# Order of the last products and place of the zero writes in a one-core transformer block

## The chip, the cores and the metric

The kernel runs on one core of one Trainium2 chip. Times are device microseconds of that core from start to end, over several runs; a profiled execution beside them leaves a trace of every instruction.

## The reference, cut to what matters

One layer on 1024 tokens of width 1024, in float32:

```
q, k, v, u = split(x @ w_in)
a = differential attention(q, k, v)      # 4 heads, softmax pairs, chunk-causal
s = S5 state-space mixer(u) with a gate  # 32 groups of 16 channels, 64 states each
h = layernorm(alpha * x + concat(a, s) @ w_out)
moe[t] = sum over the 2 experts chosen for t of  w * (silu(h @ w_gate) * (h @ w_up)) @ w_down
out = layernorm(alpha * h + moe)         # 32 experts, 4 groups, top 2 of one group
```

## The kernel before

Tokens lie in eight tiles of 128 rows (P = 128). Products are done in pairs of halves: a float32 operand is split into a high part (a cast on ACT) and a low part (a subtraction on DVE or POOL), and three products of the parts are added in PSUM.

The stages follow each other: projection of u and the constants of the state-space mixer (to some 75 us); the state-space units, with the projections of q, v and k filled in between them (`ssm_pair`, line 640); attention with the gate of the mixer and the loading of `w_out` filled in; output projection, first layernorm and routing (`route`); the 32 experts, one after the other; the last layernorm over the eight tiles.

Storage: 25 slots of 8 KB per partition are handed out by `Slots` (line 52), first released, first taken. A tile that takes a slot waits for the last reader of the slot's former tile.

Order: up to the first gather of expert rows, each engine's instructions are put in order by a planner, which simulates the program with costs of its own and issues on each engine what is ready, the earlier in the program first. From that gather on `keep_order` (line 1335) pins every engine to the order of the program. The queues of DMA issues on SP and POOL are ordered in the same way.

The zeros: the experts scatter their rows into `moe_dram`, two rows per token (2048 rows of 4 KB, 8 MB). Rows that no expert writes have to be zero. A memset on POOL (line 910) fills a tile of 128 by 1024, and four DMAs on SP's queue (line 912) write it to the 2048 rows, after attention unit 13 (`ZERO`).

The tail: experts 30 and 31 aren't scattered. Their rows are added to the sum by products with a choosing matrix. For each token tile i there are:

- `so_far` (line 1367): a load of the tile's rows of `moe_dram` by SP, then an accumulating load of its second rows by POOL, into `mos[i]`;
- `total(i)` (line 1440): the sum so far goes into PSUM by products with the identity (line 1449), then the products for expert 30 are added (line 1459);
- `add_late(i, 1)` (line 1452): the products for expert 31 (line 1455);
- `moments(i, step)` (line 1461): mean and variance. For a tile marked A in `NORM` ACT reads the sum out of PSUM (line 1472) and makes a square pass (line 1476); for a tile marked V DVE takes statistics from PSUM (line 1469). POOL makes the reciprocal root;
- `normed_rows(i, step)` (line 1481): two passes on DVE, then the tile's DMA to the output.

PSUM has eight banks: a tag `bank_pair` of two buffers of two banks each, a tag `bank0` with two buffers, and two single banks, `bank2` and `bank3`. An A tile takes a `bank_pair` buffer; a V tile takes two single banks: tile 0 both buffers of `bank0`, tile 7 `bank2` and `bank3`. Expert 31's y is in `bank0` too.

Of the kernel before, what the change touches and what calls it, by code (L numbers as in the profile page):

```python
# [11 lines left out]
F32 = mybir.dt.float32  # L12
# [7 lines left out]
P = 128  # L20
D = 1024
T = 1024
NT = T // P
# [9 lines left out]
NONE = 4096  # L33
ORDERED = (mybir.EngineType.PE, mybir.EngineType.Activation, mybir.EngineType.DVE, mybir.EngineType.Pool,
           mybir.EngineType.SP)
NORM = 'VAAAAAAV'
ZERO = 13
GB = 0
ASK, GLU, WO = (6, 12), (15, 16, 1, 20, 21, 1), (22, 24, 26, 30)
FILLS = [(ASK[0], ("ask", 2)), (ASK[1], ("ask", 3))]  # L40
for half in range(2):
    a, b, c = GLU[3 * half:3 * half + 3]
# [72 lines left out]
def tile_kernel(ctx: ExitStack, tc: tile.TileContext, I: dict, out: bass.AP, dbg=None):  # L115
    nc = tc.nc
    V, S, G, PE, SP = nc.vector, nc.scalar, nc.gpsimd, nc.tensor, nc.sync
# [7 lines left out]
    sl = Slots()  # L125
# [5 lines left out]
    def bank(name, which=0):  # L131

        if which == 1:
            turn[0] ^= 1
            which = 2 + turn[0]
        return psum.tile([P, 512], F32, tag=f"bank{which}", name=name, bufs=1 if which else 2)

    def bank2(name):
        return psum.tile([P, 1024], F32, tag="bank_pair", name=name, bufs=2)
# [6 lines left out]
    moe_dram = dram.tile([2 * T, D], F32, name="moe_dram")  # L146
# [13 lines left out]
    def add(out_, a, b, eng=V):  # L160
        return eng.tensor_tensor(out=out_, in0=a, in1=b, op=ALU.add)  # L161
# [110 lines left out]
    UTs, zT, qr, vv = {}, {}, {}, {}  # L272
# [265 lines left out]
    def wk(name, shape, bufs=1):  # L538
        return areas[where[name]].get(name, shape[1:], bufs=bufs, parts=shape[0])
# [59 lines left out]
    def ssm_unit(u, UT, z2, made):  # L599

        uo = 4 * (u % 2)
        Wm, Tm, M, C, Sn = made

        pz = bank(f"pz{u}", 1)
        for g in range(4):
            PE.matmul(pz[:, g * P:(g + 1) * P], Wm[:, g, :], UT[:, uo + g, :], start=True, stop=True)
        pz3 = pz.rearrange("p (g b) -> p g b", g=4)
        r1 = wk("r1", [P, 4, P])
        r2 = wk("r2", [P, 4, P])
        mul(r1, pz3, C)  # L610
        mul(r2[0:64], pz3[64:P], Sn[0:64])
        mul(r2[64:P], pz3[0:64], Sn[64:P])
        add(r1, r1, r2)
        Gs = wk("Gs", [P, 4, P])
        for g in range(4):
            V.tensor_tensor_scan(out=Gs[:, g, :], data0=r8[:, 4 * u + g:4 * u + g + 1].broadcast_to([P, P]),
                                 data1=r1[:, g, :], initial=0.0, op0=ALU.mult, op1=ALU.add)
        Gw = wk("r2", [P, 4, P])
        S.copy(Gw[0:64], Gs[64:P])
        S.copy(Gw[64:P], Gs[0:64])  # L620
        mul(Gs, Gs, C)
        mul(Gw, Gw, Sn)
        sub(H[:, :, 1:P], Gs[:, :, 0:P - 1], Gw[:, :, 0:P - 1])
        py = bank(f"py{u}")
        for g in range(4):
            o = py.rearrange("p (t g c) -> p t g c", g=4, c=16)[:, :, g, :]
            PE.matmul(o, UT[:, uo + g, :], Tm[:, :, g, :], start=True, stop=False)
            PE.matmul(o, H[:, g, :], M[:, g, :, :].rearrange("p t c -> p (t c)"), start=False, stop=True)

        y2 = wk("r1", [P, 512])  # L630
        k0 = math.sqrt(2.0 / math.pi)
        S.activation(y2, py, AF.Square, scale=math.sqrt(k0 * 0.044715))
        stt(y2, y2, k0, py, ALU.add, ALU.mult)
        S.activation(y2, y2, AF.Tanh)
        stt(z2[:, :, 16 * uo:16 * uo + 64], y2.rearrange("p (t n) -> p t n", t=8), 1.0,
            py.rearrange("p (t n) -> p t n", t=8), ALU.add, ALU.mult)
# [3 lines left out]
    def ssm_pair(c4, fill):  # L640
        z2 = wk("z2", [P, 8, P])
        if c4 % 2 == 0:
            zT[c4 // 2] = sl.get([P, 2, T], F32, f"zT{c4 // 2}")
        UT = UTs[c4 // 2][:, c4 % 2, :, :]
        for u in (2 * c4, 2 * c4 + 1):
            if u + 1 < NG // 4:
                made[u + 1] = ssm_prepare(u + 1)
            if u + 2 == NG // 4:
                spp.close()
                areas[0].close()  # L650
            ssm_unit(u, UT, z2, made.pop(u))
            if u + 2 == NG // 4:
                areas[1].close()
            fill(u)
        if c4 % 2 == 1:
            sl.put(UTs.pop(c4 // 2))
        for tq in range(2):
            pz = bank(f"zt{c4}{tq}", tq)
            for t_ in range(4):
                PE.transpose(pz[:, t_ * P:(t_ + 1) * P], z2[:, 4 * tq + t_, :], ident)  # L660
            S.mul(zT[c4 // 2][:, c4 % 2, :].rearrange("p (b t) -> p t b", t=8)[:, 4 * tq:4 * tq + 4, :],
                  pz.rearrange("p (t b) -> p t b", t=4), 0.5)
# [25 lines left out]
    def proj_k(h):  # L688
# [6 lines left out]
        sub(t_[64:P, 1, :], o[64:P, :], t_[0:64, 1, :].bitcast(F32))  # L695
        kk[h] = t_

    fills = [(proj_q, 0), (proj_q, 1), (proj_q, 2), (proj_q, 3), (proj_v, 0), (proj_v, 1), (proj_v, 2), (proj_v, 3)]
    made[0] = ssm_prepare(0)
    for c4 in range(4):  # L700
        ssm_pair(c4, lambda u: fills[u][0](fills[u][1]))
# [158 lines left out]
    def start(u):  # L860
        h, i = units[u]
        if i // 4 not in aoT:
            aoT[i // 4] = sl.get([P, NH, 512], F32, f"aoT{i // 4}")
        if (h, i // 4) not in grp:
            grp[h, i // 4] = (sm("L", 8, 4).rearrange("p (j c) -> p j c", c=2),
                              sm("RL", 8, 4).rearrange("p (j c) -> p j c", c=2), bank(f"po{h}_{i}", 1))
        live[u] = scores(h, i, qd[h], grp[h, i // 4][0], i % 4)
        starts[h] = starts.get(h, 0) + 1
        if starts[h] == NT:
            sl.put(*qd.pop(h), kk.pop(h))  # L870
# [23 lines left out]
    for u, (h, i) in enumerate(units):  # L894
        if u + LEAD < len(units):
            start(u + LEAD)
        L_, RL_, po_ = grp[h, i // 4]
        weigh(h, i, live.pop(u), L_, RL_, i % 4, po_)
        if u in late:
            late.pop(u)()  # L900
        ends[h, i // 4] = ends.get((h, i // 4), 0) + 1
        if ends[h, i // 4] == 4:
            late[u + LATE] = normalize(h, i // 4, po_, RL_)
        if u in fills:
            for f_, *a_ in fills[u]:
                {"ask": ask, "pre": glu_prepare, "glu": glu, "wo": wo_part}[f_](*a_)
        if u == ZERO:

            zero = sl.get([P, D], F32, "zero")
            G.memset(zero, 0.0)  # L910
            for j in range(4):
                SP.dma_start(moe_dram[512 * j:512 * j + 512, :].rearrange("(p a) n -> p a n", p=P),
                             zero.unsqueeze(1).broadcast_to([P, 4, D]))
    for f_ in late.values():
        f_()
    sl.put(zero, *vv.values())
    half.close()


# [145 lines left out]
    for pos, i in enumerate(ORDER):  # L1065
# [8 lines left out]
        o = [bank2(f"mix{i}")] if not quick else [bank2(f"mix{i}{hs.start}") for hs in HALVES]  # L1074
# [363 lines left out]
    xs, outs = {}, {}  # L1438

    def total(i):  # L1440

        if NORM[i] == "A":
            xs[i] = bank2(f"x{i}")
            o = [xs[i][:, hs] for hs in HALVES]
        else:
            o = xs[i] = [bank(f"x{i}{j}", which) for j, which in enumerate((2, 3) if i else (0, 0))]
        outs[i] = o
        for o_, hs in zip(o, HALVES):
            PE.matmul(o_, ident, mos[i][:, 0, hs], start=True, stop=False)  # L1449
        add_late(i, 0)  # L1450

    def add_late(i, j):
        for o_, hs in zip(outs[i], HALVES) if j else ():
            for v in range(2):
                PE.matmul(o_, chosen[:, j, i, :], yhl[LATE[j]][:, v, hs], start=False, stop=(v == 1))
        if j == 0:
            for v in range(2):
                for o_, hs in zip(outs[i], HALVES):
                    PE.matmul(o_, chosen[:, j, i, :], yhl[LATE[j]][:, v, hs], start=False, stop=False)

    def moments(i, step):

        x, w_ = mos[i][:, 1, :], mos[i][:, 0, :]
        sums_, r = sums[:, i, :], rstd[:, i:i + 1]
        if NORM[i] == "V":
            if step == 0:
# [8 lines left out]
        else:  # L1475
            S.activation(w_, x, AF.Square, bias=sums_[:, 2:3], scale=1.0 / 32, accum_out=sums_[:, 0:1])
        if step == (NORM[i] == "A"):
            add(r, sums_[:, 0:1] if step else sums_[:, 2:3], less[:, 2:3], G)
            G.tensor_tensor(out=r, in0=r, in1=mhalf[:, 0:1], op=ALU.pow)

    def normed_rows(i, step):
        x, w_ = mos[i][:, 1, :], mos[i][:, 0, :]
        m_ = sums[:, i, 1:2]
        if step == 0:
            if NORM[i] == "A":
                stt(w_, x, m_, lnc[:, 0, :], ALU.add, ALU.mult)
# [6 lines left out]
            (SP, S)[j].dma_start(out[0, i * P:(i + 1) * P, hs], x[:, hs])  # L1493

    for i in range(NT + 2):
        for k in (0, 1) if i == 0 else (i + 1,) if i + 1 < NT else ():
            total(k)
        if i < NT:
            add_late(i, 1)
        if 1 <= i <= NT:  # L1500
            moments(i - 1, 1)
            normed_rows(i - 1, 0)
        if i >= 2:
            normed_rows(i - 2, 1)
        if i < NT:
            moments(i, 0)
# [7 lines left out]
    with tc.For_i(0, nov, 1) as it:  # L1514
# [34 lines left out]
        for src in (w_g, w_u):  # L1549
            o = bank("ovo")  # L1550
# [66 lines left out]
```

## Time and profile before

| what | us |
|---|---|
| three runs | 1185.71, 1184.47, 1189.87; median 1185.71 |
| profiled execution | 1182.18 |
| its span | 1180.4 |
| TensorE busy | 1081.9 (92%) |
| DVE busy | 970.2 (82%) |
| ACT busy | 711.6 (60%) |
| POOL busy | 359.0 (30%) |
| four writes of zeros, from issue to landing (median) | 13.2 |

Busy time says what an engine did, not what the end waited for; that is read from the chain of waits (from the last instruction back to what released it, step by step) and from each engine's timeline, where a bracket behind a row gives the idle time before it and what ended it. The 92% of TensorE is a mean over stages. The granted clock is the share of full speed that TensorE was given: 1.00 is 2.4 GHz, 0.50 is 1.2 GHz.

### The profile page before, as it was taken

How to read it: one execution, taken by the hardware profiler on the slowest of the kernel's cores; microseconds unless marked ns; L12 is line 12 of the kernel's file. 1: busy time of each engine (PE TensorE's matmuls, PEld its weight loads, DVE VectorE, ACT ScalarE, POOL GpSimd, SP SyncE). 2: the span in 40 equal slices, each digit the busy share in tenths (PEclk: the TensorE clock that was granted, in tenths of full speed). 3: DMA queues.
4: the chain of work that ended last, by engine and by line, in shares of the span. 5: the costliest groups of instructions: out<-in, count | busy, mean ns of one | idle time of the engine just before them, and what ended most of it. 6: DMA issues, size and time to landing. Idle time of an engine off the chain costs nothing.

```text
span 1180.4 us, 15229 instructions
## 1 busy us (share of the span) xinstructions
PE 1081.9 (92%) x5345; PEld 902.0 (76%) x5345; DVE 970.2 (82%) x1430; ACT 711.6 (60%) x960; POOL 359.0 (30%) x297
## 2 busy tenths in 40 slices
PE   6979999896779899995999999999999999999983
PEld 4867887686668788884888888888888888888852
DVE  4898666657878874565999999999999999999955
ACT  3312333445656743213888888888888888888832
POOL 1087464422442643341212122122122122121122
PEclk9989999998999999995999999999999999999997
DMA  8531111211181454545699999999999999999582
GB/s 208 138 99 43 55 46 46 59 30 42 32 325 36 159 210 136 196 178 200 238 361 378 383 369 399 383 385 396 381 374 376 377 370 386 395 386 386 172 208 108
DMA packets 90622, 278.90 MB, mean 236 GB/s; under 512 B 29404, under 2 KB 49900, under 8 KB 66096
## 3 DMA queue, kind: packets, MB, share of 16 engines
q1 hardware_dynamic: 78016, 252.78, 57.1%
q0 software_dynamic: 11520, 24.83, 7.7%
q8 instruction: 43, 0.70, 0.2%
q10 hardware_dynamic: 1008, 0.30, 0.1%
q14 instruction: 35, 0.29, 0.1%
HBM read 254.12 MB, written 34.60 MB: 245 GB/s over the span
## 4 chain that ended last, share of the span: by engine, by line
PE 74%; DVE 13%; ACT 5%; DMA 3%; issue 3%; SPq 1%; POOL 1%; ACTq 0%; DVEq 0%; POOLq 0%
PE g L1246 15%; PE u L1246 14%; PE y L1237 14%; PE proj L244 8%; PE mix L1077 7%; PE xT L1207 3%; DMA misc<-in_w_in_dram 2%; ACT p L783 2%; PE glu L733 2%; PE po L818 1%; PE hT L1219 1%; PE x L1449 1%; PE pl L1099 1%; DVE ssmt L158 1%; DVE ssm L158 1%
## 5 line engine op out<-in xcount | busy, mean ns | idle before, releaser
L1146 POOL DMA_INDIRECT moe_dram<-yo,idx x30 | 52.1, 1738 | 425.9 <-DVE yo L164 425.9
L244 PE MATMUL proj<-xh,wa 128*128 128x512 f32 x256 | 75.9, 403 | 1.7 <-ACT ssm L678 1.6
L244 PE MATMUL proj<-xh,wb 128*128 128x512 f32 x256 | 73.9, 400 | 1.6 <-ACT ssm L678 1.6
L1077 PE MATMUL mix<-woh,mx 128*128 128x512 f32 x256 | 74.3, 401 | 0.7 <-ACT p L783 0.7
L1141 POOL DMA_INDIRECT gx<-h_dram,idx x32 | 60.2, 1881 | 22.5 <-DVE WT L161 13.1
L783 ACT ACTIVATE p<-s,nm 128x1024 f32<-128x1024 f32 (+7 forms) x64 | 47.3, 745 | 26.8 <-DVE nm L798 17.0
L244 PEld LDWEIGHTS proj<-xh,wa 128*128 128x128 f32 x256 | 48.6, 193 | 11.8 <-ACT ssm L678 1.8
L244 PEld LDWEIGHTS proj<-xh,wb 128*128 128x128 f32 x256 | 48.0, 191 | 11.4 <-ACT ssm L678 1.8
L1077 PEld LDWEIGHTS mix<-woh,mx 128*128 128x128 f32 x256 | 48.1, 191 | 10.5 <-ACT p L783 1.0
L1253 ACT ACTIVATE yo<-y,WT 128x1024 f32<-128x1024 f32 (+1 forms) x33 | 36.0, 1091 | 24.4 <-PE y L1237 24.4
L780 PE MATMUL s<-kk,qh 128*128 128x512 f32 (+3 forms) x96 | 38.0, 399 | 12.5 <-ACT p L783 12.2
L818 PE MATMUL po<-vv,half 128*128 128x128 f32 x288 | 43.4, 294 | 6.7 <-ACT half L815 6.6
L818 PEld LDWEIGHTS po<-vv,half 128*128 128x128 f32 x288 | 39.2, 205 | 9.9 <-ACT half L815 8.7
L1207 PEld LDWEIGHTS xT<-ident,gx 128*128 128x128 f32 x256 | 36.2, 208 | 9.9 <-DMA gx<-h_dram,idx 5.8
L1207 PE MATMUL xT<-ident,gx 128*128 128x128 f32 x256 | 36.9, 287 | 7.0 <-DMA gx<-h_dram,idx 5.6
L155 DVE TENSOR_TENSOR xe<-xT,xe 128x1024 fp32r<-128x1024 f32 (+1 forms) x33 | 39.2, 1189 | 4.3 <-ACT xe L174 4.3
L244 PE MATMUL proj<-xl,wa 128*128 128x512 f32 x128 | 42.6, 404 | 0.0
L164 DVE SCALAR_TENSOR_TENSOR yo<-gx,first,yo 128x1024 f32<-128x1024 f32 (+1 forms) x33 | 41.3, 1252 | 1.5
L1077 PE MATMUL mix<-wol,mx 128*128 128x512 f32 x128 | 42.2, 398 | 0.0
L244 PE MATMUL proj<-xl,wb 128*128 128x512 f32 x128 | 41.4, 399 | 0.0
L174 ACT CAST xe<-xT 128x1024 fp32r<-128x1024 f32 (+1 forms) x33 | 32.3, 979 | 13.6 <-PE xT L1207 13.6
L164 DVE SCALAR_TENSOR_TENSOR p<-p,rho 128x1024 f32<-128x1024 f32 (+7 forms) x32 | 36.2, 1135 | 1.0 <-DMA moe_dram<-zero 0.3
(864 smaller groups left out, 3546.7 us busy)
## 6 DMA issues: line engine op xcount, KB each, us to landing
misc<-in_w_in_dram SPq DMA_DIRECT2D x16, 512.0 KB, 3.9
moe_dram<-zero SPq DMA_DIRECT2D x4, 2048.0 KB, 13.2
xr<-in_x_dram SPq DMA_DIRECT2D x8, 512.0 KB, 8.5
wo_raw<-in_w_out_dram SPq DMA_DIRECT2D x4, 1024.0 KB, 4.8
xa<-in_x_dram SPq DMA_DIRECT2D x8, 512.0 KB, 3.5
h_dram<-xa SPq DMA_DIRECT2D x8, 512.0 KB, 3.2
mo<-moe_dram SPq DMA_DIRECT2D x8, 512.0 KB, 6.0
mo<-moe_dram POOLq DMA_DIRECT2D x8, 512.0 KB, 13.1
```

The costliest lines, as they stand in the source:

```text
L155: eng.tensor_tensor(out=out_, in0=a, in1=b, op=ALU.subtract)
L164: return V.scalar_tensor_tensor(out=out_, in0=a, scalar=s, in1=b, op0=op0, op1=op1)
L244: PE.matmul(o[:, hs], wt[kt // 4][:, w_, kt % 4, :], x_[:, hs], start=(kt == 0 and n == 0), stop=(kt == KT - 1 and n == 2))
L780: PE.matmul(s_[:, c0:c0 + w], qd[0][:, c, tk], kk[h][:, c, c0:c0 + w], start=True, stop=False)
L783: S.activation(p_[:, c, 0:n], s_[:, 0:n], AF.Exp, bias=nm[:, c:c + 1], accum_out=L[:, j, c:c + 1])
L818: PE.matmul(po[:, j * P:(j + 1) * P], aT[:, k, :], vv[k // 4][:, k % 4, h * P:(h + 1) * P], start=(k == 0), stop=(k == i))
L1077: PE.matmul(o[-(hs.start > 0)][:, hs], mx[:, m_, kt, :], (woh, wol)[w_][kt // 2][:, kt % 2, hs], start=(kt == 0 and n == 0), stop=(kt == K ...
L1141: return G.indirect_dma_start(out=dst, out_offset=None, in_=h_dram[:, :], in_offset=bass.IndirectOffsetOnAxis(ap=ix, axis=0), bounds_check ...
L1146: G.indirect_dma_start(out=moe_dram[:, :], out_offset=bass.IndirectOffsetOnAxis(ap=ix, axis=0), in_=src, in_offset=None, bounds_check=2 * ...
L1207: PE.transpose(b_[:, kt * P:(kt + 1) * P], rows(g_, kt), ident)
L1237: PE.matmul(y[h_], hid[e][:, x_, kt, :], w_[:, k, HALVES[h_]], start=(kt == 0 and n == 0), stop=(kt == 3 and n == 2))
L1246: PE.matmul(o, xT[e][:, x_, kt, :], w_[:, k, :], start=(kt == 0 and n == 0), stop=(kt == KT - 1 and n == 2))
```

## The change

In the tail, the products of expert 31 for tile i are put ahead of `total(i+1)` in the program, except for the first two totals. The fourth tile (tile 3) is normed in the V way and takes the two buffers of `bank0`; tiles 0 and 7 take `bank2` and `bank3`. The zeros are written by eight DMAs of 1 MB instead of four of 2 MB; their place in the program is behind the first four state-space units, two to a unit, with the memset and its slot ahead of the first unit. The slot is given back after the fourth unit.

```diff
-NORM = 'VAAAAAAV'
-ZERO = 13
+NORM = 'VAAVAAAV'
...
             fill(u)
+            zeros(u)
...
+    zero = sl.get([P, D], F32, "zero")
+    G.memset(zero, 0.0)
+
+    def zeros(u):
+        for j in range(2 * u, 2 * u + 2) if u < ZU else ():
+            SP.dma_start(moe_dram[256 * j:256 * j + 256, :].rearrange("(p a) n -> p a n", p=P),
+                         zero.unsqueeze(1).broadcast_to([P, 2, D]))
+        if u == ZU - 1:
+            sl.put(zero)
+
+    ZU = 4
...
-        if u == ZERO:
-
-            zero = sl.get([P, D], F32, "zero")
-            G.memset(zero, 0.0)
-            for j in range(4):
-                SP.dma_start(moe_dram[512 * j:512 * j + 512, :].rearrange("(p a) n -> p a n", p=P),
-                             zero.unsqueeze(1).broadcast_to([P, 4, D]))
...
-    sl.put(zero, *vv.values())
+    sl.put(*vv.values())
...
-            o = xs[i] = [bank(f"x{i}{j}", which) for j, which in enumerate((2, 3) if i else (0, 0))]
+            o = xs[i] = [bank(f"x{i}{j}", which) for j, which in enumerate((0, 0) if i == 3 else (2, 3))]
...
-        for k in (0, 1) if i == 0 else (i + 1,) if i + 1 < NT else ():
-            total(k)
+        if i == 0:
+            total(0)
+            total(1)
         if i < NT:
             add_late(i, 1)
+        if 0 < i < NT - 1:
+            total(i + 1)
```

## Rows read from the trace of the kernel before

**Rows 1.** Chain of waits, tail: start us, us, what ran.

```profile
1133.98 1.72 PE x L1449 x4
...
1138.76 1.98 PE x L1449 x4
1140.74 0.93 PE x L1459 x4
...
1142.66 0.90 issue
...
1143.80 1.98 PE x L1449 x4
```

**Rows 2.** Wait table, TensorE, 1110 to 1165: total us, times, longest.

```profile
PE x L1449 <- ACT mo L1472: 4.8, 4, 1.2
```

**Rows 3.** Timelines in the tail: start us, us, engine, line, operation [idle before].

```profile
1126.44 1.02 PE L1449 MATMUL x<-mo,ident 128*128 128x512 f32 x2
...
1129.80 0.69 DVE L155 TENSOR_TENSOR yhl<-yo,yhl 128x512 fp32r<-128x512 f32 x1 [0.69 <-ACT yhl L1256]
...
1137.59 1.02 ACT L1472 ACTIVATE mo<-x 128x1024 f32<-128x1024 f32 x1 [7.82 <-PE x L1455]
...
1140.07 0.19 ACT L1476 ACTIVATION_READ_ACCUMULATOR mo<-mo,sums 128x1 f32 x1
...
1161.32 1.03 ACT L1472 ACTIVATE mo<-x 128x1024 f32<-128x1024 f32 x1 [0.91 <-PE x L1455]
...
1164.10 0.19 ACT L1476 ACTIVATION_READ_ACCUMULATOR mo<-mo,sums 128x1 f32 x1
...
1164.32 1.31 DVE L164 SCALAR_TENSOR_TENSOR mo<-mo,sums,lnc 128x1024 f32<-128x1024 f32 x1 [1.36 <-ACT mo L1476]
1165.55 1.27 DVE L164 SCALAR_TENSOR_TENSOR mo<-mo,rstd,lnc 128x1024 f32<-128x1024 f32 x1
1166.74 1.28 DVE L1469 BATCH_NORM_STATS2 st<-x 128x6 f32<-128x512 f32 x2
...
1169.63 2.60 DVE L164 SCALAR_TENSOR_TENSOR mo<-mo,rstd,lnc 128x1024 f32<-128x1024 f32 x3
```

**Rows 4.** DMA issues near 1119.06 and 1133.79: count, KB, us to landing.

```profile
mo<-moe_dram POOLq DMA_DIRECT2D x1, 512.0 KB, 15.8
...
mo<-moe_dram POOLq DMA_DIRECT2D x1, 512.0 KB, 11.0
```

**Rows 5.** POOL's timeline: last accumulating load, the zero memset, state-space stage.

```profile
1133.79 0.87 POOL L1373 DMA_DIRECT2D mo<-moe_dram  x1 [2.96 <-DMA mo<-moe_dram]
...
323.20 0.95 POOL L910 MEMSET zero<- 128x1024 f32 x1 [4.60 <-PE s L780]
...
73.53 2.23 POOL L158 TENSOR_TENSOR ssm<-ssmp 128x512 f32<-128x512 f32 x2 [3.45 <-DVE ssmp L155]
```

**Rows 6.** Stretches: us, busy PE, PEld, DVE, ACT, POOL, granted clock, DMA share, GB/s.

```profile
336.00:338.00 2.00, 0.14 (x1) 0.14 (x2) 1.96 (x3) 0.00 (x0) 0.72 (x1) 1.00 1.03 422
...
82.00:86.00 4.00, 0.72 (x4) 0.72 (x5) 3.97 (x5) 0.62 (x1) 3.84 (x3) 0.50 0.48 136
```

**Rows 7.** SP's timeline of DMA issues, start of the kernel.

```profile
13.08 0.77 SPq L282 DMA_DIRECT2D B<-in_ssm_b_re_dram  x1
...
40.25 0.34 SPq L262 DMA_DIRECT2D u_dram<-ut  x1
...
70.17 0.34 SPq L262 DMA_DIRECT2D u_dram<-ut  x1
80.99 0.39 SPq L191 DMA_DIRECT2D misc<-in_w_in_dram  x1
```

**Rows 8.** Timelines of ACT and TensorE around the first state-space units.

```profile
85.23 0.62 ACT L174 CAST wa<-misc 128x512 fp32r<-128x512 f32 x1 [14.45 <-DMA misc<-in_w_in_dram]
87.52 0.21 ACT L575 COPY ssm<-pk 128x64 f32<-128x64 f32 x1 [1.67 <-PE pk L570]
...
94.29 1.05 PE L606 MATMUL pz<-UT,ssm 128*128 128x128 f32 x8
```

## The prediction

> **What bounds the kernel now.** I read the page's shares first, then the chain of work that ended last, then the wait table and each engine's timeline in the two places that the change touches: the tail (from the last expert product to the end, some 54 us), and 70 to 350 us, where the zeros are written. TensorE is busy over 90% of the span, but that is a mean over stages. In the expert stage, nearly half of the span, the order is pinned and nothing of the change falls there.
>
> In the tail the chain runs through TensorE and one ACT instruction in turn [rows 1]: four identity products (1.72 us, or 1.98 where they start after a wait), four of expert 30 (0.93), four of expert 31 (0.93), then ACT's read of the finished tile (0.90 and what ends it), and only then the next identity products. The period from 1138.76 to 1143.80 is 5.04 us, of which TensorE works 3.84; four starts of this kind stand in the chain with that spacing. The wait table names it: x waits for ACT 4 times, 4.8 us in all [rows 2]. The reader is to see there that the cause is order: `total(i+1)` stands ahead of `add_late(i, 1)`, and for an ACT tile it needs the double bank that ACT's read of tile i-1 gives back. So TensorE stands in that wait with products of tile i still to do, and ACT can't start on tile i either.
>
> **The tail, step by step.** After the change `add_late(i, 1)` comes first. ACT reads tile i while TensorE does `total(i+1)`, whose bank was given back one tile earlier. TensorE's work per tile is 1.72 + 0.93 + 0.93 = 3.58 us if nothing makes it wait.
>
> - Start: tile 0 moves from the two bank0 buffers, which expert 31's y holds until ACT has read it, to banks 2 and 3, whose last reader (the split of expert 31's hidden tile) is over before y can start. Its products start at 1126.44, as now, and don't stop half-way: totals 0 and 1 end at 1126.44 + 2 x 2.65 = 1131.74. Expert 31's last split is done by 1129.80 + 0.69 = 1130.49 [rows 3], so `add_late(0, 1)` follows at once, to 1132.67, and `add_late(1, 1)` to 1133.6.
> - Then one tile per 3.58 us: `add_late(6, 1)` ends at 1133.6 + 5 x 3.58 = 1151.5, tile 7's last product at 1155.1. Before, ACT's read of tile 6 started at 1161.32.
> - ACT from there to the end of tile 6's square pass: 2.97 us now for tile 6 (1161.32 to 1164.29), 2.67 for tile 1 (1137.59 to 1140.26, [rows 3]). I take 2.7: 1154.2, against 1164.29.
> - DVE from there on works without a gap, 1164.32 to 1172.23, 7.9 us [rows 3]: tile 6's first pass, tile 5's second, tile 7's statistics, three more passes. It comes to tile 7 at its third step, 2.42 us in (1156.6), after 1155.1. End: 1154.2 + 7.9 = 1162.1.
>
> Gain: 1172.23 - 1162.1 = **10.1 us**. What follows (output, drain) has the same length.
>
> Can the others keep that pace? An ACT tile costs DVE 1.23 + 1.19 = 2.42 us, a statistics tile 1169.63 - 1166.74 + 1.2 = 4.1 (starts in [rows 3]). Three of these (0, 3 and 7) and five of those are 24.4 us, against 8 x 3.58 = 28.6 for TensorE. Walked tile by tile, DVE is up to 2 us late with the fourth tile, which is now its own, and has caught up at tile 4's first pass. What is late next is the data: every tile needs its accumulating load. Tile 3's took longest, 15.8 us from 1119.06, so it landed at 1134.9; the last landed at 1133.79 + 11.0 = 1144.8 [rows 4, 5]. Tile 3 is wanted at 1137.2, tile 7 at 1151.5. I put nothing on it; by the same working the margin of the first tiles is only 1 to 2 us, so -7 bounds the tail on that side. On the other, -10.5: ACT and POOL a little quicker than taken.
>
> **The zeros.** Removed at unit 13: one memset (0.95 us, behind a 4.60 us wait for its slot, [rows 5]) and four DMAs of 2 MB. The chain there goes through scores, ACT and DVE, not through POOL. I take 0; bounds: -4.6 (all of POOL's wait counts) to +4.6 (the planner orders the attention anew, and as much is lost).
>
> Added in the state-space stage: a memset (0.95) and eight DMAs of 1 MB. The memset's slot was `ut3`. POOL waits for 3.45 us before 73.53 [rows 5], which covers it; without that cover, 0.95. The DMAs need only the memset. SP's order is the planner's, and it puts a ready load far ahead of its place in the program: line 282 at 13.08, before line 262 at 40.25 [rows 7]. SP issues nothing between the store at 70.17 (0.34) and the weight load at 80.99, so I expect most of the eight there, not two to a unit. They move 8.4 MB; at 422 GB/s, the rate while the old ones ran [rows 6], 20 us in which all DMA engines are full, from 74 to 94.
>
> Queued behind them on SP: that weight load, the small copies of line 582, the 4 KB loads of line 577. ACT's cast of the weights waits in order, 14.45 us, until 85.23; behind it stand the copies for the next unit at 87.52, which TensorE reads at 94.29 [rows 8]. If all eight lie in front, the weights land at some 94 + 1.3 = 95.4, ten us later, the copies come at 96.5 to 97.5, and TensorE loses 3.2. If they are spread, each pair is 5 us of transfer, and the wait of 14.45 us is longer than that. I take the middle, **+1.5**; bounds 0 and +20 (every transfer exposed).
>
> The Trainium skill's page "DMA: Bandwidth & Descriptors", section "Queues, rings and completion order", says that SP's DMAs share one row of rings and that each ring takes its descriptors in order, so a load issued behind the zeros starts behind them. By that rule the bunch costs the full 3.2 and the sum is 1.7 worse. No row here shows a load behind the zeros on SP's queue.
>
> The slots that follow shift by one, since the zero tile holds none during attention: each later tile gets a slot that was released no later. 0, or 2 either way.
>
> Sum: -10.1 + 1.5 = -8.6. The profiled execution took 1182.18 (span 1180.4), so 1173.6. It lies 3.5 under the median of the runs, 1185.71; on that median **1177.1**.
>
> **The rivals.** A measurement of this kernel can tell about 0.5%, 5.9 us, from no change.
> - *Half of the zeros exposed*: the tail as computed, +10 between 75 and 140 us. Sum about 0: 1186. For it: ACT waits there for loads on SP's queue now. Against: TensorE's weights come a projection ahead, and it has a gap there anyway (0.72 us busy of the 4 from 82, [rows 6]).
> - *Slower*: the zeros stand ahead of every weight load, and ACT, in order, holds up the unit's chain. From 16 us exposed of the 20 it decides (16 - 10.1 = 5.9), and TensorE then runs on at half clock, as now from 82 to 86 (granted 0.50, [rows 6]): 20 + 4 - 10 = +14, 1200. Against: in that window POOL and DVE are full, so the gap belongs to them and not to a DMA.
> - *The tail gains less*: the accumulating loads set the pace, or DVE falls behind after tile 3: -7 + 1.5, so 1180. For it: margins of 1 to 2 us at the first tiles.
> - *The attention gains too*: POOL's 4.6 counts: 1172.5.
>
> **How the numbers follow.** Forecast (1172 to 1181 by itself) 0.64; tail gains less 0.11; attention gains too 0.06; half exposed 0.13; slower 0.06. Faster (under 1179.8) takes nearly all of the first, the third, half of the second and little of the fourth: 0.78. Same: 0.16; slower: 0.06. The range 1169.5 to 1183 leaves out the slower case, most of the half exposed, and little at the lower end.
>
> **What would show it.** In the changed trace: identity products that don't wait for ACT's read; a period near 3.6 us; ACT's last square pass and DVE's last eight instructions some 10 us nearer to the last y product; statistics on DVE for three tiles. Of the zeros: all eight on SP before 85, and ACT's cast at 85.23 later by up to ten. If the expert stage starts more than 5 us later than now, or the identity products wait for their loads, the prediction is wrong by that much.

## The result, and the profile after

The changed kernel takes 1177.78 us (median of five, 1174.69 to 1178.66), the one before 1185.71 (five, 1183.66 to 1189.87): ratio 0.9933, 95% interval 0.9916 to 0.995. The forecast was 1177.1. The profiled execution took 1178.13 (span 1176.4), 4.0 less than the one before. So the two traces stand 4.0 apart and the medians 7.9, and it matters below which of the two a difference is taken from.

The end first. This is TensorE's timeline of the changed kernel (start us, us, engine, line, operation; lines have moved: identity products 1454, expert 30's products 1464, expert 31's 1460):

```profile
1131.04 1.88 PE L1454 MATMUL x<-mo,ident 128*128 128x512 f32 x4
1132.35 1.50 PE L1464 MATMUL x<-yhl,chosen 128*128 128x512 f32 x4
1133.68 1.88 PE L1454 MATMUL x<-mo,ident 128*128 128x512 f32 x4
1135.00 1.49 PE L1464 MATMUL x<-yhl,chosen 128*128 128x512 f32 x4
1136.33 1.99 PE L1460 MATMUL x<-yhl,chosen 128*128 128x512 f32 x8
1138.16 1.88 PE L1454 MATMUL x<-mo,ident 128*128 128x512 f32 x4
...
1152.43 1.88 PE L1454 MATMUL x<-mo,ident 128*128 128x512 f32 x4
1153.74 1.50 PE L1464 MATMUL x<-yhl,chosen 128*128 128x512 f32 x4
1155.08 1.09 PE L1460 MATMUL x<-yhl,chosen 128*128 128x512 f32 x4
1156.00 1.88 PE L1454 MATMUL x<-mo,ident 128*128 128x512 f32 x4
...
1158.65 1.08 PE L1460 MATMUL x<-yhl,chosen 128*128 128x512 f32 x4
```

No row has a wait. A tile costs 3.57 us (1152.43 to 1156.00), where it cost 5.04 [rows 1]; the row "x waits for ACT" of [rows 2] has gone. ScalarE, however, has a new one. Its timeline for the last two tiles that it norms:

```profile
1152.63 1.02 ACT L1477 ACTIVATE mo<-x 128x1024 f32<-128x1024 f32 x1 [0.24 <-PE x L1460]
1153.55 0.19 ACT L1477 ACTIVATION_READ_ACCUMULATOR mo<-x 128x1 f32 x1
1155.16 1.15 ACT L1481 ACTIVATE mo<-mo,sums 128x1024 f32<-128x1024 f32 x1 [1.42 <-POOL sums L157]
1156.22 0.19 ACT L1481 ACTIVATION_READ_ACCUMULATOR mo<-mo,sums 128x1 f32 x1
1156.31 1.00 ACT L1477 ACTIVATE mo<-x 128x1024 f32<-128x1024 f32 x1
1157.22 0.19 ACT L1477 ACTIVATION_READ_ACCUMULATOR mo<-x 128x1 f32 x1
1159.04 1.15 ACT L1481 ACTIVATE mo<-mo,sums 128x1024 f32<-128x1024 f32 x1 [1.63 <-POOL sums L157]
1160.09 0.19 ACT L1481 ACTIVATION_READ_ACCUMULATOR mo<-mo,sums 128x1 f32 x1
```

Between a tile's reading pass and its square pass ScalarE stands idle for 1.42 and 1.63 us, until GpSimd has made the negative mean out of the sum. GpSimd's timeline shows why that takes so long:

```profile
1156.48 0.19 POOL L160 TENSOR_TENSOR rstd<-sums,less 128x1 f32<-128x1 f32 x1 [1.35 <-ACT mo L1481]
1156.75 1.40 POOL L1484 TENSOR_TENSOR rstd<-rstd,mhalf 128x1 f32<-128x1 f32 x1
1158.13 0.88 POOL L157 TENSOR_TENSOR sums<-sums,less 128x2 f32<-128x2 f32 x1
```

The sum was there at 1157.41 (1157.22 + 0.19), but the power that belongs to the tile before ran until 1158.13, and in its queue it stands first. Beside that power of 1.40 us VectorE was at work, as the first two rows here show; below the dots stand a power that took 0.55 us and, above it, VectorE's row beside it:

```profile
1156.44 1.31 DVE L163 SCALAR_TENSOR_TENSOR mo<-mo,sums,lnc 128x1024 f32<-128x1024 f32 x1 [1.36 <-ACT mo L1481]
1157.67 1.27 DVE L163 SCALAR_TENSOR_TENSOR mo<-mo,rstd,lnc 128x1024 f32<-128x1024 f32 x1
...
1164.30 1.41 DVE L163 SCALAR_TENSOR_TENSOR mo<-x,sums,lnc 128x512 f32<-128x512 f32 x2
1164.61 0.55 POOL L1484 TENSOR_TENSOR rstd<-rstd,mhalf 128x1 f32<-128x1 f32 x1
```

In the ends of the fourteen traces of this case the power took 1.40 to 1.48 us all 73 times that VectorE was in a pass from `mo` to `mo` meanwhile, and 0.55 to 0.57 us all 39 times that it wasn't. For a tile that ScalarE norms, the same square pass releases both, so they run together. No run moved one away from the other, so it is not shown that VectorE's pass causes the delay.

From one square pass to the next it is 3.88 us (1155.16 to 1159.04), against TensorE's 3.57. From the first identity product to the end of VectorE's last pass, the end was 1126.44 to 1172.23 before, 45.8 us [rows 3]; it is 1131.04 to 1168.23, 37.2 us. **The end gained 8.6 us.**

In the profiled pair 4.6 of these are lost again ahead of it: the first identity product comes at 1131.04 instead of 1126.44. The zeros went out on SP as these rows of its timeline show (issue times, not transfers):

```profile
94.49 5.58 SPq L704 DMA_DIRECT2D moe_dram<-zero  x5
100.18 9.87 SPq L581 DMA_DIRECT2D ssm<-ssm  x8
110.09 0.59 SPq L576 DMA_DIRECT2D ssm<-in_ssm_d_dram  x1
110.72 0.57 SPq L704 DMA_DIRECT2D moe_dram<-zero  x1
111.39 0.56 SPq L190 DMA_DIRECT2D misc<-in_w_in_dram  x1
111.99 2.27 SPq L704 DMA_DIRECT2D moe_dram<-zero  x2
```

Five in a bunch, then one and two, from 94 to 114 us. TensorE loses nothing while they run; it falls behind later. Stretches of the kernel before, then of the changed one (columns as in [rows 6]):

```profile
180.00:200.00 20.00, 19.32 (x113) 16.52 (x111) 14.51 (x25) 7.71 (x13) 7.88 (x7) 1.00 0.16 40
200.00:225.00 25.00, 19.57 (x112) 16.35 (x112) 16.11 (x21) 13.71 (x19) 11.14 (x10) 0.99 0.28 69
225.00:250.00 25.00, 24.21 (x113) 19.84 (x112) 19.28 (x26) 7.48 (x11) 5.78 (x4) 0.95 0.10 24
```

```profile
180.00:200.00 20.00, 18.36 (x94) 15.47 (x92) 14.21 (x23) 6.27 (x11) 7.53 (x6) 0.91 0.14 36
200.00:225.00 25.00, 19.90 (x104) 16.46 (x102) 13.25 (x17) 9.73 (x14) 11.97 (x11) 0.86 0.16 39
225.00:250.00 25.00, 19.45 (x94) 15.91 (x94) 17.26 (x21) 10.14 (x16) 5.80 (x4) 0.93 0.23 55
```

63.1 us of TensorE's work became 57.7, the granted clock fell (2.4 GHz throughout would be 1.00), and the first scores start at 272.7 instead of 264.0. No zero is written there any more. What differs is the order: with the zeros in another place the planner orders all engines anew, from the first units of the state-space stage on. Whether the order or the writes cost the time is tried below.

### The profile page after: what moved, and what is told of

It reads as the page before. It is cut to its first block, busy times and chain, and to the rows that moved or that the text cites. A ratio compares the mean times of both kernels' runs of the same rounds, so it can differ in the third digit from the quotient of the medians.

```text
span 1176.4 us, 15227 instructions
## 1 busy us (share of the span) xinstructions
PE 1083.7 (92%) x5345; PEld 903.9 (77%) x5345; DVE 970.0 (82%) x1434; ACT 708.5 (60%) x956; POOL 358.0 (30%) x296
## 4 chain that ended last, share of the span: by engine, by line
PE 69%; DVE 12%; DMA 7%; ACT 4%; SPq 3%; issue 3%; POOL 1%; ACTq 0%; DVEq 0%; POOLq 0%
PE g L1251 15%; PE y L1242 15%; PE u L1251 14%; PE mix L1082 7%; PE proj L243 4%; DMA misc<-in_w_in_dram 3%; PE xT L1212 3%; DMA moe_dram<-zero 2%; PE glu L745 2%; PE po L830 2%; DVE ssm L157 1%; SPq L581 1%; PE hT L1224 1%; PE s L792 1%; PE pl L1104 1%
## 5 line engine op out<-in xcount | busy, mean ns | idle before, releaser
L830 PE MATMUL po<-vv,half 128*128 128x128 f32 x288 | 41.0, 285 | 1.4 <-ACT half L827 1.3
L830 PEld LDWEIGHTS po<-vv,half 128*128 128x128 f32 x288 | 37.4, 198 | 3.5 <-ACT half L827 2.4
L792 PEld LDWEIGHTS s<-kk,qh 128*128 128x128 f32 x96 | 19.3, 201 | 24.7 <-ACT p L795 22.6
```

The source lines that it names most:

```text
L792: PE.matmul(s_[:, c0:c0 + w], qd[0][:, c, tk], kk[h][:, c, c0:c0 + w], start=True, stop=False)
L830: PE.matmul(po[:, j * P:(j + 1) * P], aT[:, k, :], vv[k // 4][:, k % 4, h * P:(h + 1) * P], start=(k == 0), stop=(k == i))
```

## The experiments

The theory at the start was: the end is worth 8.6 us; the zeros' move costs below 1 us in the median, and the 4.6 us of the profiled pair are the planner's new order. The rival: the writes themselves cost those 4.6 us. Each ratio is to the kernel before on the same chip; ratios from different chips are compared only through it, and their 95% intervals are some 2 to 3 us to either side.

**The end alone** (kernel before with the three edits of the end, zeros as they were), and once more on another chip (two of the three edits are shown; the third is the banks of the V tiles):

```diff
-NORM = 'VAAAAAAV'
+NORM = 'VAAVAAAV'
...
+        if 0 < i < NT - 1:
+            total(i + 1)
```

> The kernel before with the change's end alone (last products ahead of the next tile's identity products, fourth tile normalised on VectorE in single banks); the zeros stay where they were, in one piece at unit 13. Theory A: the end is worth what the two traces show, from the first identity product to VectorE's last pass 45.8 us before and 37.2 after, 8.6 us; the zeros' move costs little in the median (below 1 us), and the 4.6 us by which the profiled runs differ ahead of the end is a new order of the planner's. Then this kernel is 7.5 to 9 us below the one before, about 1177.5, and within 1.5 us of the changed kernel. Rival: the zeros' writes among the state-space stage's loads and copies cost the 4.6 us that the profiled runs show, and the end alone would give more than the whole change: 12 us or more below the kernel before, about 1173.

> The kernel with the new end alone once more, as the yardstick of the three others on their chip: 0.991 to 0.993 of the kernel before.

Measured: 0.9917 (0.9895 to 0.9939) and 0.9914 (0.9891 to 0.9937) of the kernel before, 9.8 to 10.2 us less; the end 37.0 and 36.4 us long. That is more than the 7.5 to 9 expected and less than the rival's 12; in the traces the end is 8.8 and 9.4 us shorter, and the difference lies inside the intervals.

**The zeros alone** (changed kernel with the old end):

> The changed kernel with the old end: only the zeros' move is left of the change. Theory A: between -1 and +2 us against the kernel before, and its end again 45.8 us long, with its first identity product within 5 us of either trace's. Rival (the writes cost what the profiled runs differ by): +4 to +5 us, about 1190.

Measured: 1.0032 (1.0015 to 1.005), 3.8 us more (1.8 to 6); the end 45.8 us long again, the first scores at 273.0. The expectation of at most 2 was missed by the median, and the interval holds the rival's 4 to 5 as well: the move has a price that can be measured, though by the ratios the whole change lies only 1.5 to 1.9 us above the end alone (0.9933 and, run again, 0.9927), which is inside their intervals. Whether the writes or the new order are that price, this run can't say.

**The products' order alone** (fourth tile still on ScalarE, banks as before):

> The kernel before with only the order of the products in the end changed; the fourth tile stays on ScalarE, in a pair of banks, and the second tile-kind's bank stays as it was. Theory A: the products' order takes away TensorE's waits, but ScalarE then has six tiles of 3.9 us (read and square pass, in the changed kernel's trace) against TensorE's 3.57, with no tile in the middle to catch up on, so its last square pass ends 1 to 3 us later than in the changed kernel: 5.5 to 7.5 us below the kernel before. Rival 1: the order is the whole gain, -8 to -9. Rival 2: the fourth tile's place is the main part, and the order alone gives at most 3 us.

Measured: 0.9934 (0.9915 to 0.9953), the end 38.8 us long: by the traces 7.0 us of the gain are the order, some 1.6 to 2.5 the fourth tile and the banks. (By the times it is 7.8 us, between theory A and rival 1, and the interval overlaps with that of the end alone; the split rests on the traces.) The trace has both parts of the smaller share: TensorE still waits once for bank0, and ScalarE, without a tile to catch up on, ends its last square pass at 1161.83, 1.0 us after TensorE's last product instead of 0.5.

```profile
1132.88 1.12 PE L1449 MATMUL x<-mo,ident 128*128 128x512 f32 x2 [0.93 <-ACT yo L1253]
...
1160.59 1.15 ACT L1476 ACTIVATE mo<-mo,sums 128x1024 f32<-128x1024 f32 x1 [1.63 <-POOL sums L158]
1161.65 0.18 ACT L1476 ACTIVATION_READ_ACCUMULATOR mo<-mo,sums 128x1 f32 x1
```

**The mean on ScalarE** (changed kernel, and later the end alone with it):

```diff
-            mul(sums_[:, 1:3], sums_[:, 0:1].broadcast_to([P, 2]), less[:, 0:2], G)
+            S.mul(sums_[:, 2:3], sums_[:, 0:1], -1.0 / (32 * D))
+            S.mul(sums_[:, 1:2], sums_[:, 0:1], -1.0 / D)
```

> The changed kernel, with the two small products that turn a tile's sum into its negative mean made on ScalarE itself, right after its reading pass, rather than on GpSimd behind the power of the tile before. Theory A: what the end lost against the forecast (37.2 us instead of 35.7) is ScalarE's square pass waiting for GpSimd (1.6 us for the last tile); with the sum's products on ScalarE, two of about 0.2 to 0.3 us, the last square pass ends about 1 us earlier and so does VectorE's end: -0.7 to -1.5 us against the changed kernel. Rival: VectorE is the bound of the end (its tiles of 3.3 us and three last passes), and nothing changes: within 0.3 us of the changed kernel.

> The new end alone (zeros at unit 13 as before) and the two small products of a tile's mean on ScalarE rather than on GpSimd. Both gains are in different instructions, so they should add: the end 35.6 us long instead of 45.8, and the time 1.0 to 1.4 us below the kernel with the new end alone, about 1172; if the mean's gain was a scatter of runs, no difference.

ScalarE's timeline of the first:

```profile
1155.25 1.02 ACT L1477 ACTIVATE mo<-x 128x1024 f32<-128x1024 f32 x1 [0.86 <-PE x L1460]
1156.17 0.20 ACT L1477 ACTIVATION_READ_ACCUMULATOR mo<-x 128x1 f32 x1
1156.39 0.20 ACT L1479 ACTIVATE sums<-sums 128x1 f32<-128x1 f32 x1
1156.50 0.19 ACT L1480 ACTIVATE sums<-sums 128x1 f32<-128x1 f32 x1
1156.72 1.15 ACT L1482 ACTIVATE mo<-mo,sums 128x1024 f32<-128x1024 f32 x1
1157.78 0.19 ACT L1482 ACTIVATION_READ_ACCUMULATOR mo<-mo,sums 128x1 f32 x1
```

The wait for GpSimd is gone; from the read's start to the square pass's end it is 2.72 us, not 3.97, and ScalarE waits for TensorE again. The end is 35.8 us long in both traces: 1.4 less than in the changed kernel, 0.6 to 1.1 less than in the two traces of the end alone. The times don't show it: 0.994 (0.992 to 0.996) beside 0.9933 for the changed kernel, and 0.992 (0.9895 to 0.9945) beside 0.9917 and 0.9914 for the end alone, where 1.0 to 1.4 us less were expected. So the version is shorter in its traces and unproven in its times; that it beats the kernel before is the end's doing.

**Order and transfers apart.** Two kernels fill the other corners. In one each engine is held to the order that it has in the changed kernel, the zeros' buffer is still taken and given back, but the writes are at unit 13 again. In the other the order of the kernel before is held, and the eight writes stand where the changed kernel has them on SP. Each instruction ahead of the experts got a dependency on the one that went before it on its engine:

```diff
+            for i in seq:
+                if prev is not None:
+                    tc.add_manual_dep(i, prev.name, ..., reason="pin_front")
+                prev = i
```

> The changed kernel with the zeros written at unit 13 again (from a small constant tile), while each engine's order of work ahead of the experts is held as it came out in the changed kernel, and the buffer that the zeros took in the state-space stage is still taken, zeroed and given back. So only the transfers leave the state-space stage. Theory O (the new order and the shifted buffers cost it, not the transfers): about the changed kernel's time, 1176 to 1179, with the first scores near 272 us again. Theory T (the 8 MB of writes among the stage's loads and copies cost it): as the kernel with the new end alone, about 1173.5, the first scores near 264.

> The other corner: the kernel with the new end alone, its engines' order ahead of the experts held as it was and its buffers as they were, but the zeros written in eight pieces during the state-space stage (from a small constant tile of 512 bytes a partition), at the places in SP's queue where the changed kernel has them. Theory O: as the kernel with the new end alone, 1172.5 to 1175, the first scores within 2 us of 264. Theory T: 3 to 5 us more, 1177 or above, the loss to be seen between 100 and 130 us, where the pieces are under way.

> The changed kernel itself once more, on the chip of the three others, as their yardstick: 0.993 of the kernel before, 1175 to 1178; 3 to 5 us above the kernel with the new end alone if the zeros' move costs what its own run showed.

Measured on one chip: the new order without the transfers 0.9932 (0.9909 to 0.9954), the changed kernel 0.9927 (0.9899 to 0.9956), the old order with the transfers **1.0125** (1.0096 to 1.0153). So neither theory held as put. In the new order the transfers cost nothing that can be told, to within some 3 us; in the trace without them the first scores stand at 269.5, between the two groups of kernels, so the late scores need not be the order alone. In the old order they cost 25 us against the end alone. (The old order held with the zeros at unit 13 was not run; that holding costs nothing by itself is seen in the new order only.) The second kernel had written from a small tile, in pieces of 512 bytes, so one more run took that difference away:

> The kernel with the new end alone, its engines' order held and its buffers as they were, the zeros written in the state-space stage at the changed kernel's places in SP's queue and in the changed kernel's pieces of 4 KB a row (from a buffer that is free just then). It differs from the small-piece kernel, which lost 30 us against the new end alone, in the size of the pieces only. Theory P (the small pieces made that stall: 286 GB/s instead of 406): within 3 us of the kernel with the new end alone. Theory T (what stands behind 8 MB in SP's queue waits for them, and the changed kernel escaped it by its new order): the writes take some 20 us instead of 28, and the loss is 8 to 20 us.

Measured: 1.0036 (1.002 to 1.0052), beside 0.9914 for the end alone on the same chip: 14.5 us. (Against the end alone the small pieces had cost 25 us, not the 30 of that text.) So size is some 10 of the 25, and the stall is real. By the traces (275.8 against 267.3, 560.8 against 547.0) 8.5 us are lost by the first scores and 13.8 by the first gather; what costs the rest in between stays open. ScalarE's timeline in this kernel, then in the end alone, where the writes come later:

```profile
104.67 0.63 ACT L636 ACTIVATE ssm<-ssm 128x512 f32<-128x512 f32 x1 [0.75 <-DVE ssm L166]
117.94 0.62 ACT L176 CAST wb<-misc 128x512 fp32r<-128x512 f32 x1 [12.64 <-DMA misc<-in_w_in_dram]
121.32 0.62 ACT L621 COPY ssm<-ssm 64x512 f32<-64x512 f32 x1 [2.77 <-DVE ssm L618]
```

```profile
104.70 0.63 ACT L634 ACTIVATE ssm<-ssm 128x512 f32<-128x512 f32 x1 [1.70 <-DVE ssm L164]
109.12 0.62 ACT L174 CAST wb<-misc 128x512 fp32r<-128x512 f32 x1 [3.79 <-DMA misc<-in_w_in_dram]
116.07 0.62 ACT L619 COPY ssm<-ssm 64x512 f32<-64x512 f32 x1 [6.33 <-DVE ssm L616]
```

The same cast stands ahead of the same copies, and its weights come 8.8 us later. 6.1 of these are not transfer: SP issues that load at 111.22 instead of 105.17, since it was held up with the small copies ahead of it (9.89 us for eight, 5.00 without the zeros). From issue to landing it is 2.8 more. In the changed kernel the planner has put two copies for the next unit ahead of the casts:

```profile
113.43 0.62 ACT L618 COPY ssm<-ssm 64x512 f32<-64x512 f32 x1 [8.93 <-DVE LI L984]
114.06 0.62 ACT L619 COPY ssm<-ssm 64x512 f32<-64x512 f32 x1
...
118.18 1.14 ACT L173 CAST wb<-misc 128x512 fp32r<-128x512 f32 x2 [1.98 <-DMA misc<-in_w_in_dram]
```

The weights land as late (the cast starts at 118.18 against 117.94), but the copies came at 113.43 instead of 121.32, and TensorE's work for the unit, which waits for them, goes on: its products for y start at 117.65 there and at 129.28 in the held order. **That is the step by which, in the traces, the new order avoids this stall;** it was not tried by itself.

**Does attention regain time because the zeros hold no buffer there?** The kernels in the new order reach the first scores some 7 us late and the first gather about 2 us late. To try it, the end alone with the zeros still in the attention stage, but from a constant tile of 512 bytes; and the mean on ScalarE with it:

```diff
-            zero = sl.get([P, D], F32, "zero")
-            G.memset(zero, 0.0)
+            with tc.issue_after(gl_["load"].ins):
...
+                    SP.dma_start(moe_dram[512 * j:512 * j + 512, :].rearrange("(p a) (b n) -> p (a b) n", p=P, n=128),
+                                 zc.unsqueeze(1).broadcast_to([P, 32, 128]))
```

> The kernel with the new end alone, with the zeros still written in the attention stage (behind the w_glu load) but from a small constant tile, so that they take none of the attention's buffers; the order in the state-space stage stays as before. The changed kernels come to the first scores 7 us later than the others (272 against 265) and to the first gather only 1 us later: attention regains 6. Theory B (it regains them because the zeros no longer take a buffer there): first scores near 265 and first gather near 541, 4 to 6 us below the kernel with the new end alone. Rival (attention has slack for a late start, whatever the buffers): within 1.5 us of it.

> The kernel of the run before with the mean's two small products on ScalarE as well: the end 35.8 us long instead of 37.0, so 1.0 to 1.4 us below it; by theory B about 0.986 of the kernel before, by the rival about 0.991.

Measured: 0.9972 (0.9952 to 0.9991) and 0.9959 (0.994 to 0.9978): 5 to 7 us *slower* than the end alone. The first scores are at 264.3, as hoped, and the first gather at 554.8. The loss lies at 330 to 360 us, where TensorE is busy for 19.7 us instead of 24.7 and the small pieces are under way. So the theory gained nothing, but the run doesn't refute it either, since pieces of that size were seen to cost by themselves in the old order. They don't cost it everywhere: in the kernel with the new order and the writes at unit 13 the same pieces go out from 328.5, and TensorE is busy for 25.1 of those 30 us. The mean on ScalarE gives 1.5 us between these two, by ratios whose intervals overlap. Why attention regains those 5 us stays open.

The kernels in one view (times of the traces, us; the end from the first identity product to VectorE's last pass):

| kernel | of before | first scores | first gather | end starts | end long |
|---|---|---|---|---|---|
| before | 1 | 264.0 | 545.2 | 1126.4 | 45.8 |
| changed, its two traces | 0.9933, 0.9927 | 272.7, 271.5 | 549.2, 549.7 | 1131.0, 1131.7 | 37.2, 37.2 |
| end alone, its two | 0.9917, 0.9914 | 264.6, 267.3 | 545.0, 547.0 | 1126.8, 1128.3 | 37.0, 36.4 |
| order alone | 0.9934 | 265.6 | 548.4 | 1130.9 | 38.8 |
| end alone, mean on ScalarE | 0.9920 | 265.7 | 550.4 | 1131.9 | 35.8 |
| zeros alone | 1.0032 | 273.0 | 549.1 | 1131.2 | 45.8 |
| changed, mean on ScalarE | 0.9940 | 271.8 | 548.2 | 1130.1 | 35.8 |
| new order, writes at unit 13 | 0.9932 | 269.5 | 544.2 | 1126.7 | 36.8 |
| old order, writes early, 4 KB | 1.0036 | 275.8 | 560.8 | 1141.9 | 36.4 |
| old order, writes early, 512 B | 1.0125 | 286.6 | 569.8 | 1151.3 | 37.5 |
| end alone, zeros from a constant tile | 0.9972 | 264.3 | 554.8 | 1136.6 | 37.4 |
| the same, mean on ScalarE | 0.9959 | 265.2 | 552.4 | 1133.5 | 35.8 |

One trace's start of the end scatters by 5 us among kernels with the same order in front (1126.4 to 1131.9), so the 4.6 us of the profiled pair lie within scatter; the first scores (264.0 to 267.3 with the old place of the zeros, 271.5 to 273.0 with the new) do not.

## Why the prediction was right, step by step

- **What bounds the tail**: right. The order made TensorE wait, and the order alone took 7.0 of the 8.6 us in the traces.
- **TensorE's pace**: right. From the first identity product to the end of tile 6's products the working has 25.1 us (1126.44 to 1151.5) and the trace 25.1 (1131.04 to 1156.17); to tile 7's last product 28.7 and 28.7. The accumulating loads cost nothing, though the margin had been put at 1 to 2 us.
- **ScalarE after that**: the term that was mis-sized. 2.7 us were taken, 4.1 measured (1156.17 to 1160.28). The prediction had asked of VectorE and of the loads whether they keep the new pace, and put GpSimd among what may be "a little quicker". Its queue was the one that didn't: at one tile in 3.57 us the next sum comes while the power of the tile before still runs. In the wait table of before that wait had stood with 0.6 us at most (`ACT mo L1476 <- POOL sums L158: 2.1, 6, 0.6`: total us, times, longest). With the mean on ScalarE the changed kernel's end is 1.4 us shorter, nearly the whole shortfall of 1.5 (10.1 forecast, 8.6 by the trace).
- **VectorE's last 7.9 us**: right, 7.92 (1160.31 to 1168.23).
- **Zeros in the state-space stage, +1.5**: small, as forecast, but rather too small (3.8 by themselves, 1.8 at the least; 1.5 to 1.9 between the whole change and the end alone, inside their intervals), and wrong in how. Not all eight stood before 85: the memset ran at 85, as GpSimd got to it, and the first write at 94.49, so ScalarE's cast at 85.23 [rows 8] moved by nothing (85.19). And the stall that the prediction worked out, a cast that waits for weights behind the zeros with the next unit's copies behind it, is there one unit later; but it is what the *old* order pays, as part of 14.5 us. The prediction kept the order of before in mind, where the planner made another.
- **The two rivals with exposed zeros** (+10 and +20 us in front) describe what the held old order paid, and its 14.5 us lies between them; in the changed kernel they did not come true, for a reason that neither had named.
- **The ring rule** of the Trainium skill's page "DMA: Bandwidth & Descriptors", section "Queues, rings and completion order", is that each ring takes its descriptors in order; no row could be shown for it. The trace agrees: the 4 KB copies, first of their unit, landed 7.9 us after their issue (median of two in the changed kernel), against 1.7 where no zeros are ahead. The 3.2 us that the prediction drew from it can't be told from its own +1.5 by the times (3.8, 1.8 to 6), but the way was another: the cast at 85.23 was not behind the zeros.
- **The sum**: -8.6 was forecast, -7.9 came in the medians (-8.7 by the ratio when it was run again). By its trace the end gained 1.5 less than forecast, by the times of the end alone (9.8 to 10.2) about what was forecast; the zeros cost 3.8 by themselves instead of 1.5; and base and front scatter by more than any of these. That both agree so closely is partly luck.

## What to carry to other kernels

When a wait is taken out of a pipelined end, ask of every engine that a tile passes, the small helpers too, whether it keeps the new pace in its queue's order; here a power of one column came to hold ScalarE up. A transfer that is moved is judged by what stands behind it on its issue queue, and who stands behind that on the engine that waits; where a planner makes the order, look at the new order before pricing the old one. To part a planner's answer from the edit itself, hold each engine's order and run the corners.

## What the runs showed of the hardware

- Small transfers behind large ones held up the issuing engine too: the eight copies of a unit took SP 9.87 us to issue behind five writes of 1 MB, 5.00 without them.
- The same 8 MB of zeros went at 403 to 409 GB/s in rows of 4 KB and at 285 to 293 in rows of 512 bytes, all DMA engines being full (share 1.02 to 1.06) either way; four issues of 2 MB took SP 4.7 to 6.4 us in the one form and 22.4 to 22.7 in the other.
- GpSimd's power of one column took 0.55 us in some places and 1.40 in others of the same end, the product of two columns 0.19 and 0.87. It was the longer value for every power that ran beside a pass of VectorE from `mo` to `mo` (73 of 112), and the shorter one for all others; of the products, 31 that took 0.49 to 0.88 ran beside such a pass, and of the 27 that took 0.20 or less only one overlapped with one, for 0.2 us. That the pass is the cause was not tried.
